# Rotary embedding on a full DMA queue: groups of four batches, half-row tiles, and one PSUM tile for two rows

## The chip, the cores and the metric

The kernel runs on one core of a Trainium2 chip. The metric is the device time of one execution in microseconds; the kernel before takes 162.35 us in the median of 10 runs (162.23 to 162.76).

## The reference

The input x has 16 batches of 512 positions of 1024 numbers in float32. The 1024 numbers are 16 heads of 64, and a head is two halves of 32. Each position has 32 cosines and 32 sines, which all batches and heads share.

```python
x = x.reshape(batch, seq, num_heads, head_dim)
x1, x2 = (x[..., :half_dim].copy(), x[..., half_dim:].copy())
cos = cos[None, :, None, :].copy()
sin = sin[None, :, None, :].copy()
rotated = np.concatenate([x1 * cos - x2 * sin, x1 * sin + x2 * cos], axis=-1)
```

So every output element is its own input times a cosine plus the element of the other half times a sine with a sign: two products and a sum for each of 8.4 million elements, 33.5 MB in and 33.5 MB out.

## The kernel before

**Tiles.** A tile is two batches (`NB = 2`): partition p holds 8 consecutive positions ("rows" of 1024 numbers) of one batch, 32 KB in one piece in memory and on the chip. There are 8 tiles of 4 MB. Five of them have a place on the chip at once, in buffers for 1, 2 and 2 tiles (`HOMES`); results overwrite the input in place. Tiles 5, 6 and 7 reuse the places of 0, 1 and 2.

**Transfers.** All but one are issued by SP, in program order, on one queue; sin is issued by ACT. First come three rows of tile 0, cos, the other five rows (`FIRST`), tile 1, tile 2, and tiles 3 and 4 in one. After that `stores(t)` at the end of each tile issues what is due: store t, except that tiles 3 and 4 go out together after tile 4; after tile 2 also the load of tile 5 and a load of 6 and 7 together. A DMA that must wait for an engine or for an earlier DMA holds up all that is behind it on SP.

**Tables.** cos and sin come in on 64 partitions and are spread to both batches by a matmul with a 0/1 matrix (`spread`, L121 and L122). `sns` holds each sine with both signs in on-chip memory (L124, L125); the cosines stay in PSUM (`tab`). `own_t` is a copy of row 0's signed sines in PSUM.

**The work on a tile** is written out by hand in order (`manual_schedule`), and each engine executes its instructions in that order. The eight rows go three ways:
- Rows 1-2, 4-5 and 6-7 are the pairs. DVE multiplies a pair with the cosines into the PSUM tile `pd` (L149, `pair_product`), POOL multiplies the swapped halves with the sines into a buffer b (L173, `sin_rows`), and DVE adds the two into x (L197, `pair_sum`). There is one `pd`, of four banks, and so a pair's sum must be done before the next pair's product.
- Row 0: DVE writes the cosine product into the PSUM tile `own_ps` (one tile ahead), multiplies the row by the sines in place (L158, `own_product`); TensorE adds the swapped row to `own_ps` by matmuls with the identity (L184, `pe_add`); ACT copies `own_ps` to x (L217).
- Row 3 (`ROW_PE`) goes in two halves through a PSUM tile of its own, `pe_ps`: DVE's product of 512 (L149), TensorE's addition of POOL's product b3 (L184), ACT's copy (L189), all in `pe_half`.

On DVE a tile is this sequence: product of pair 1, own product, sum of pair 1, first half of row 3, product of pair 2, sum of pair 2, second half of row 3, product of pair 3, row 0's product of the next tile, sum of pair 3. Buffers b come from one pool of three, which also held the tables at the start.

[...]

Of the kernel before, what the change touches and what calls it, by code (L numbers as in the profile page):

```python
# [12 lines left out]
NB = 2  # L13

HOMES = (1, 2, 2)
BANK = 512
# [6 lines left out]
FIRST = (3, 8)  # L23
# [3 lines left out]
def kernel(  # L27
# [12 lines left out]

    nc = tc.nc
# [6 lines left out]
    KK = seq // PB  # L48
    NT = batch // NB
    F = KK * dim  # L50

    x_v = x.rearrange("(t b) (p k) d -> t (b p) (k d)", b=NB, k=KK)
    out_v = out.rearrange("(t b) (p k) h d -> t (b p) (k h d)", b=NB, k=KK)
    cos_v = cos.rearrange("(p k) j -> p (k j)", k=KK)
    sin_v = sin.rearrange("(p k) j -> p (k j)", k=KK)
# [3 lines left out]
    bp = ctx.enter_context(tc.tile_pool(name="bp", bufs=3))  # L59
    pfix = ctx.enter_context(tc.tile_pool(name="pfix", bufs=1, space=bass.MemoryType.PSUM))  # L60
# [4 lines left out]

    homes = [xp.tile([P, n, F], FP32, name=f"x{n}{i}") for i, n in enumerate(HOMES)]
    places = [home[:, i] for home, n in zip(homes, HOMES) for i in range(n)]
    tiles = [places[t % len(places)] for t in range(NT)]
    first_of = [sum(HOMES[:i]) for i in range(len(HOMES))]

    def both(t):

        return homes[first_of.index(t % len(places))]

    def load(t, lo=0, hi=KK):
        s = slice(lo * dim, hi * dim)
        nc.sync.dma_start(out=tiles[t][:, s], in_=x_v[t][:, s])

    def load_two(t):
        nc.sync.dma_start(out=both(t), in_=x_v[t : t + 2].rearrange("t p f -> p t f"))  # L80

    def store(t):
        nc.sync.dma_start(out=out_v[t], in_=tiles[t])  # L83

    def store_two(t):
        nc.sync.dma_start(out=out_v[t : t + 2].rearrange("t p f -> p t f"), in_=both(t))

    tabs = bp.tile([P, 2 * dim], FP32, name="b")
    sin_sb = tabs[:PB, : KK * half]
    cos_sb = tabs[:PB, dim : dim + KK * half]  # L90
    nc.scalar.dma_start(out=sin_sb, in_=sin_v)
    load(0, 0, FIRST[0])
    nc.sync.dma_start(out=cos_sb, in_=cos_v)
    for lo, hi in zip(FIRST, FIRST[1:]):
        load(0, lo, hi)
    load(1)
    load(2)
    load_two(3)
# [3 lines left out]
    for _ in range(2):  # L102
        nc.gpsimd.nop(hint="pause")
# [3 lines left out]
    pe_ps = pe.tile([P, BANK], FP32)  # L107
    for ps in (own_ps[:, :BANK], own_ps[:, BANK:], pe_ps):
        nc.tensor.matmul(out=ps, lhsT=zero[:, :P], rhs=zero, start=True, stop=True)  # L109

    sns = fixed.tile([P, KK, 2, half], FP32)
    tab = pfix.tile([P, BANK], FP32)
    cos_t = tab[:, : KK * half]
    sin_t = pd.tile([P, 2 * dim], FP32, name="pd")[:, : KK * half]
# [8 lines left out]
    sin_k = sin_t.rearrange("p (k j) -> p k j", k=KK)  # L123
    nc.vector.tensor_scalar_mul(out=sns[:, :, 0, :], in0=sin_k, scalar1=-1.0)  # L124
    nc.vector.tensor_copy(out=sns[:, :, 1, :], in_=sin_k)  # L125
    own_t = tab[:, KK * half : KK * half + hd]
    nc.vector.tensor_copy(out=own_t, in_=sns[:, ROW_OWN])
# [8 lines left out]
    def rows(t, k, n=1):  # L136
        return tiles[t][:, k * dim : (k + n) * dim]

    def cos_product(out, r, k, n=1):

        c = cos_t[:, k * half : (k + n) * half]
        m = r.shape[1] // (n * half)
        if n == 1:
            cb = bass.AP(tensor=c.tensor, offset=c.offset, ap=[c.ap[0], [0, m], [1, half]])
            o, i = (z.rearrange("p (a j) -> p a j", j=half) for z in (out, r))
        else:
            cb = bass.AP(tensor=c.tensor, offset=c.offset, ap=[c.ap[0], [half, n], [0, m], [1, half]])
            o, i = (z.rearrange("p (k a j) -> p k a j", k=n, j=half) for z in (out, r))
        nc.vector.tensor_tensor(out=o, in0=i, in1=cb, op=ALU.mult)  # L149

    def own_product(r):

        s = bass.AP(
            tensor=own_t.tensor,
            offset=own_t.offset + half,
            ap=[own_t.ap[0], [0, nh], [-half, 2], [1, half]],
        )
        nc.vector.tensor_tensor(out=heads(r), in0=heads(r), in1=s, op=ALU.mult)  # L158

    def sin_product(out, r, k, n):  # L160
# [14 lines left out]
    def sin_rows(t, k, n):  # L175
        b = bp.tile([P, 2 * dim], FP32, name="b")[:, : n * dim]
        sin_product(b, rows(t, k, n), k, n)
        return b
# [7 lines left out]
    def pe_half(k, r, b):  # L186
        cos_product(pe_ps, r, k)
        pe_add(pe_ps, b)
        nc.scalar.copy(out=r, in_=pe_ps)  # L189

    def pair_product(t, k):
        ps = pd.tile([P, 2 * dim], FP32, name="pd")
        cos_product(ps, rows(t, k, 2), k, 2)
# [5 lines left out]
    def stores(t):  # L199
        if t == 4:  # L200
            store_two(3)
        elif t != 3:
            store(t)
        if t == 2:
            load(5)
            load_two(6)

    cos_product(own_ps, rows(0, ROW_OWN), ROW_OWN)
    for t in range(NT):
        first, second, third = PAIRS  # L210
        b1 = sin_rows(t, first[0], 2)
        p1 = pair_product(t, first[0])
        r0 = rows(t, ROW_OWN)
        own_product(r0)
# [6 lines left out]
        h0, h1 = zip(parts(rows(t, ROW_PE)), parts(b3))  # L221
        pe_half(ROW_PE, *h0)
        p2 = pair_product(t, second[0])
        b1 = sin_rows(t, third[0], 2)
        pair_sum(*p2, b2)
        pe_half(ROW_PE, *h1)
        p1 = pair_product(t, third[0])
        if t + 1 < NT:
            cos_product(own_ps, rows(t + 1, ROW_OWN), ROW_OWN)
# [37 lines left out]
```

## Time and profile before

| | |
|---|---|
| median of 10 runs | 162.35 us |
| the profiled execution's own time | 162.4 us |
| its span, first to last instruction | 160.6 us |
| DVE busy | 136.4 us (85%) |
| POOL busy | 127.0 us (79%) |
| PE busy / ACT busy | 60.9 us / 18.8 us |
| moved by DMA | 67.25 MB, 419 GB/s over the span |
| DVE pair products, L149, 24 of 128x2048 | 2291 ns each |
| DVE pair sums, L197, 24 of 128x2048 | 2287 ns each |
| POOL products, L173, 24 of 128x2048 and 8 of 128x1024 | 4524 and 2354 ns each |
| DVE products into own_ps and own products, 8 of each | 1224 and 1214 ns each |
| DVE half products of row 3, 16 | 686 ns each |
| ACT copies of row 0 and of half of row 3 | 1012 and 586 ns each |

A line of a group or of the timeline names the line of the kernel, the engine, the operation, the tile written and the tiles read, and the shapes. In a timeline the first number is the start and the second the duration in us; "x3" says that several instructions are merged in a line, and brackets hold the idle time of the engine before it and what ended it. "SPq" is SP's queue of instructions that issue DMAs. In the view of 40 slices each digit is the busy share of a fortieth of the span in tenths. Instructions of one engine overlap by up to 0.1 us at their ends, so the distance from start to start is what counts on a busy engine: 2.20 us for a pair's product or sum, 1.13 for a full row, 0.60 for a half row.

### The profile page before, as it was taken

Reading aid. Unit: us, or ns where it says so; the run is one execution under the profiler, and the core shown is the slowest. Engines: PE = TensorE matmul, PEld = TensorE weight load, DVE = VectorE, ACT = ScalarE, POOL = GpSimd, SP = SyncE. Lnnn points to the kernel's source line nnn. Section 1 sums busy time; section 2 is a strip of 40 time slices with the busy share of each in tenths; the row PEclk is TensorE's granted clock in tenths of the full one; section 3 lists DMA queues with packets and bytes.
Section 4 is the critical chain, followed back from the end, with each engine's and each line's share of the span. In section 5 each row is a group of like instructions: output and inputs, shape, how many; then the busy total and the mean of one; then the engine's idle time right before and its main releaser. Section 6 shows DMA issues by size and latency. Waiting matters only on the chain.

```text
span 160.6 us, 431 instructions
## 1 busy us (share of the span) xinstructions
PE 60.9 (38%) x71; PEld 19.2 (12%) x71; DVE 136.4 (85%) x85; ACT 18.8 (12%) x25; POOL 127.0 (79%) x38
## 2 busy tenths in 40 slices
PE   3043904074505740393119330844057502922000
PEld 0112200030102110220013000300021101210000
DVE  1079879999999999999999999998999999998000
ACT  0003211003100300021101210031003010211000
POOL 1059999999999999988998699982999999960000
PEclk9999995558655675558555955586556755585555
DMA  5999999999999999999999999999999999999993
GB/s 178 410 418 463 400 490 416 392 457 457 392 424 473 408 400 498 408 392 484 424 400 457 449 400 424 482 392 416 482 408 408 482 416 408 473 424 400 441 457 147
DMA packets 2561, 67.25 MB, mean 419 GB/s; under 512 B 256, under 2 KB 384, under 8 KB 384
## 3 DMA queue, kind: packets, MB, share of 16 engines
q1 hardware_dynamic: 2480, 67.18, 97.9%
q10 hardware_dynamic: 80, 0.07, 0.1%
q14 instruction: 1, 0.01, 0.0%
HBM read 33.69 MB, written 33.55 MB: 419 GB/s over the span
## 4 chain that ended last, share of the span: by engine, by line
DVE 43%; DMA 34%; issue 7%; POOL 7%; PE 1%; DVEq 0%; SPq 0%
DVE x L197 21%; DVE pd L149 18%; DMA x<-in_x_dram 18%; DMA out_dram<-x 12%; POOL b L173 7%; DMA b<-in_sin_dram 4%; DVE pe_ps L149 2%; PE pd L121 1%; DVE sns L124 0%; DVE sns L125 0%; DVE own_ps L149 0%; DVE x L158 0%; DVEq L197 0%; SPq L80 0%; SPq L83 0%
## 5 line engine op out<-in xcount | busy, mean ns | idle before, releaser
L173 POOL TENSOR_TENSOR b<-x,sns 128x2048 f32<-128x2048 f32 (+1 forms) x32 | 126.3, 3982 | 15.4 <-DVE sns L125 8.4
L197 DVE TENSOR_TENSOR x<-pd,b 128x2048 f32<-128x2048 f32 x24 | 54.9, 2287 | 2.3 <-POOL b L173 1.5
L149 DVE TENSOR_TENSOR pd<-x,tab 128x2048 f32<-128x2048 f32 x24 | 55.0, 2291 | 0.2
L184 PE MATMUL own_ps<-x,ident 128*128 128x512 f32 x32 | 30.2, 1100 | 54.7 <-DVE x L158 49.7
L184 PE MATMUL pe_ps<-b,ident 128*128 128x512 f32 x32 | 28.9, 1005 | 23.7 <-DVE pe_ps L149 23.7
L184 PEld LDWEIGHTS own_ps<-x,ident 128*128 128x128 f32 x32 | 9.4, 324 | 74.4 <-DVE x L158 60.5
L217 ACT COPY x<-own_ps 128x1024 f32<-128x1024 f32 x8 | 8.1, 1012 | 74.7 <-PE own_ps L184 74.7
L189 ACT COPY x<-pe_ps 128x512 f32<-128x512 f32 x16 | 9.4, 586 | 38.0 <-PE pe_ps L184 38.0
L184 PEld LDWEIGHTS pe_ps<-b,ident 128*128 128x128 f32 x32 | 8.4, 287 | 42.7 <-DVE pe_ps L149 34.1
L149 DVE TENSOR_TENSOR pe_ps<-x,tab 128x512 f32<-128x512 f32 x16 | 11.0, 686 | 0.0
L149 DVE TENSOR_TENSOR own_ps<-x,tab 128x1024 f32<-128x1024 f32 x8 | 9.8, 1224 | 0.5 <-DMA x<-in_x_dram 0.4
L158 DVE TENSOR_TENSOR x<-x,tab 128x1024 f32<-128x1024 f32 x8 | 9.7, 1214 | 0.0
L124 DVE TENSOR_SCALAR sns<-pd 128x256 f32<-128x256 f32 x1 | 0.4, 425 | 7.3 <-PE pd L121 7.3
L121 PE MATMUL pd<-b,spread 64*128 64x256 f32 x2 | 1.2, 696 | 5.0 <-DMA b<-in_sin_dram 5.0
L217 ACT ACT_TABLE_LOAD x1 | 1.3, 1283 | 14.6 <-DVE x L158 14.6
L109 PE MATMUL own_ps<-zero 128*128 128x512 bf16 x2 | 1.0, 620 | 1.2 <-DVE zero L105 1.2
L121 PEld LDWEIGHTS pd<-b,spread 64*128 64x128 f32 x2 | 0.5, 306 | 5.9 <-issue 5.9
L122 PE MATMUL tab<-b,spread 64*128 64x256 f32 x2 | 1.1, 631 | 0.0
L105 DVE MEMSET zero<- 128x256 uint32 x1 | 0.3, 272 | 0.9 <-PEq L248 0.9
L122 PEld LDWEIGHTS tab<-b,spread 64*128 64x128 f32 x2 | 0.7, 333 | 0.2
L109 PE MATMUL pe_ps<-zero 128*128 128x512 bf16 x1 | 0.6, 634 | 0.0
L109 PEld LDWEIGHTS <-zero 128*128 128x128 bf16 x3 | 0.3, 122 | 1.5 <-DVE zero L105 1.2
(9 smaller groups left out, 1.8 us busy)
## 6 DMA issues: line engine op xcount, KB each, us to landing
out_dram<-x SPq DMA_DIRECT2D x6, 4096.0 KB, 22.1
x<-in_x_dram SPq DMA_DIRECT2D x2, 8192.0 KB, 39.1
x<-in_x_dram SPq DMA_DIRECT2D x3, 4096.0 KB, 27.9
out_dram<-x SPq DMA_DIRECT2D x1, 8192.0 KB, 33.3
x<-in_x_dram SPq DMA_DIRECT2D x1, 2560.0 KB, 12.0
x<-in_x_dram SPq DMA_DIRECT2D x1, 1536.0 KB, 6.5
b<-in_sin_dram ACTq DMA_DIRECT2D x1, 64.0 KB, 6.8
b<-in_cos_dram SPq DMA_DIRECT2D x1, 64.0 KB, 6.6
```

What stands on the lines that cost most here:

```text
L105: nc.vector.memset(zero, 0.0)
L109: nc.tensor.matmul(out=ps, lhsT=zero[:, :P], rhs=zero, start=True, stop=True)
L121: nc.tensor.matmul(out=sin_t, lhsT=spread, rhs=sin_sb, start=True, stop=True)
L122: nc.tensor.matmul(out=cos_t, lhsT=spread, rhs=cos_sb, start=True, stop=True)
L124: nc.vector.tensor_scalar_mul(out=sns[:, :, 0, :], in0=sin_k, scalar1=-1.0)
L149: nc.vector.tensor_tensor(out=o, in0=i, in1=cb, op=ALU.mult)
L158: nc.vector.tensor_tensor(out=heads(r), in0=heads(r), in1=s, op=ALU.mult)
L173: nc.gpsimd.tensor_tensor(out=o, in0=i, in1=sb, op=ALU.mult)
L184: nc.tensor.matmul(out=ps, lhsT=ident, rhs=other, start=False, stop=True, skip_group_check=True)
L189: nc.scalar.copy(out=r, in_=pe_ps)
L197: nc.vector.tensor_tensor(out=r, in0=ps, in1=b, op=ALU.add)
L217: nc.scalar.copy(out=r0, in_=own_ps)
```

## The change

A group is now four batches (`NB = 4`), so that a partition has 16 consecutive rows (64 KB in one piece in memory), and a tile is one half of them: tile t is half t % 2 of group t // 2. There are again 8 tiles of 8 rows per partition, 4 MB each. The places are five slots in one buffer `xt`, so that the two tiles of a group lie side by side.

- Transfers: all on SP. Three rows of tile 0, sin, cos, five rows of tile 0, tile 1, tiles 2 and 3 in one, tile 4. Stores: tiles 0 and 1 in one after tile 1, then 2, 3, 4, 5 and 6 alone, and the last in two pieces of four rows (`LAST_OUT`). After tile 2 the load of tile 5 and of 6 and 7 in one, as before.
- Tables: sin and cos have buffers of their own, on 32 partitions, and 512 columns; the spreading matmuls are 512 wide. The second half of `sns` is written by ACT, not by DVE. The cosines fill a bank; `own_t`, for both halves of a group, is in a bank of its own and is written inside tile 0 after the first pair product.
- `pe_ps` and `pe_half` are gone. Row 3 goes whole through `own_ps`, after row 0 of the same tile and before row 0 of the next: one product of 1024, four matmul passes, one copy. On DVE it comes after the product of pair 2.
- The buffers b are two pools: three for pairs, two for row 3.
- The two pauses on POOL at the start and one of three zeroing matmuls are gone.

```diff
-NB = 2
-
-HOMES = (1, 2, 2)
+NB = 4
+SLOTS = 5
...
-FIRST = (3, 8)
+FIRST = 3
+LAST_OUT = 4
...
-    KK = seq // PB
-    NT = batch // NB
+    KK = seq // PB // 2
+    NT = 2 * batch // NB
...
-    x_v = x.rearrange("(t b) (p k) d -> t (b p) (k d)", b=NB, k=KK)
+    x_v = x.rearrange("(g b) (p k) d -> g (b p) (k d)", b=NB, k=2 * KK)
...
+    b1p = ctx.enter_context(tc.tile_pool(name="b1p", bufs=2))
...
+    xt = xp.tile([P, SLOTS * F], FP32)
+
+    def run(t, lo=0, hi=KK):
+
+        a, b = (t % SLOTS) * F, (t % 2) * F
+        return xt[:, a + lo * dim : a + hi * dim], (t // 2, slice(None), slice(b + lo * dim, b + hi * dim))
...
-    tabs = bp.tile([P, 2 * dim], FP32, name="b")
-    sin_sb = tabs[:PB, : KK * half]
-    cos_sb = tabs[:PB, dim : dim + KK * half]
-    nc.scalar.dma_start(out=sin_sb, in_=sin_v)
-    load(0, 0, FIRST[0])
+    load(0, 0, FIRST)
+    sin_sb = fixed.tile([PB, BANK], FP32)
+    cos_sb = fixed.tile([PB, BANK], FP32)
+    nc.sync.dma_start(out=sin_sb, in_=sin_v)
     nc.sync.dma_start(out=cos_sb, in_=cos_v)
-    for lo, hi in zip(FIRST, FIRST[1:]):
-        load(0, lo, hi)
+    load(0, FIRST, KK)
     load(1)
-    load(2)
-    load_two(3)
+    load(2, 0, 2 * KK)
+    load(4)
...
-    for _ in range(2):
-        nc.gpsimd.nop(hint="pause")
...
-    pe_ps = pe.tile([P, BANK], FP32)
-    for ps in (own_ps[:, :BANK], own_ps[:, BANK:], pe_ps):
+    for ps in (own_ps[:, :BANK], own_ps[:, BANK:]):
...
-    sns = fixed.tile([P, KK, 2, half], FP32)
-    tab = pfix.tile([P, BANK], FP32)
-    cos_t = tab[:, : KK * half]
-    sin_t = pd.tile([P, 2 * dim], FP32, name="pd")[:, : KK * half]
+    sns = fixed.tile([P, 2 * KK, 2, half], FP32)
+    cos_t = pfix.tile([P, BANK], FP32)
+    own_t = pfix.tile([P, 2, hd], FP32)
+    sin_t = pd.tile([P, 2 * dim], FP32, name="pd")[:, :BANK]
...
-    nc.vector.tensor_copy(out=sns[:, :, 1, :], in_=sin_k)
-    own_t = tab[:, KK * half : KK * half + hd]
-    nc.vector.tensor_copy(out=own_t, in_=sns[:, ROW_OWN])
+    nc.scalar.copy(out=sns[:, :, 1, :], in_=sin_k)
...
-        b = bp.tile([P, 2 * dim], FP32, name="b")[:, : n * dim]
-        sin_product(b, rows(t, k, n), k, n)
+        b = (bp if n == 2 else b1p).tile([P, n * dim], FP32, name=f"b{n}")
+        sin_product(b, t, k, n)
...
-    def pe_half(k, r, b):
-        cos_product(pe_ps, r, k)
-        pe_add(pe_ps, b)
-        nc.scalar.copy(out=r, in_=pe_ps)
...
     def stores(t):
-        if t == 4:
-            store_two(3)
-        elif t != 3:
+        if t == 1:
+            store(0, 0, 2 * KK)
+        elif t == NT - 1:
+            store(t, 0, LAST_OUT)
+            store(t, LAST_OUT, KK)
+        elif t > 1:
             store(t)
         if t == 2:
             load(5)
-            load_two(6)
+            load(6, 0, 2 * KK)
...
         p1 = pair_product(t, first[0])
+        if t == 0:
+            nc.vector.tensor_copy(out=own_t, in_=sns[:, ROW_OWN::KK].rearrange("p k a j -> p k (a j)"))
         r0 = rows(t, ROW_OWN)
-        own_product(r0)
+        own_product(t, r0)
...
         pair_sum(*p1, b1)
-        h0, h1 = zip(parts(rows(t, ROW_PE)), parts(b3))
-        pe_half(ROW_PE, *h0)
         p2 = pair_product(t, second[0])
+        cos_product(own_ps, t, ROW_PE)
+        for ps, b in zip(parts(own_ps), parts(b3)):
+            pe_add(ps, b)
+        nc.scalar.copy(out=rows(t, ROW_PE), in_=own_ps)
         b1 = sin_rows(t, third[0], 2)
         pair_sum(*p2, b2)
-        pe_half(ROW_PE, *h1)
         p1 = pair_product(t, third[0])
         if t + 1 < NT:
-            cos_product(own_ps, rows(t + 1, ROW_OWN), ROW_OWN)
+            cos_product(own_ps, t + 1, ROW_OWN)
```

## The prediction

> **What bounds the kernel now.** I read the page's 40 slices first, then the DMA queues, then what the SP queue waited for, and last the timeline of one tile and of the start. The DMA row of the slices is full between the first and the last:
>
> ```profile
> DMA  5999999999999999999999999999999999999993
> ...
> q1 hardware_dynamic: 2480, 67.18, 97.9%
> ```
>
> One queue carries 67.18 MB and its packets fill 97.9% of the span on all 16 engines. The packet records of the trace give 1.213 us for a 32 KB packet. The last stores landed at 140.40, 150.07 and 159.75 us: 9.68 us for each 4 MB tile, end to end. So 16 tile transfers fill some 155 us of 160.6; what is left is the start (first packet at 1.73), its ramp, and the 0.83 us after the last landing. The compute engines do not set the end, but they are close behind:
>
> ```profile
> 114.95 33.36 SPq L83 DMA_DIRECT2D out_dram<-x  x3
> ...
> 145.61 2.29 DVE L197 TENSOR_TENSOR x<-pd,b 128x2048 f32<-128x2048 f32 x1
> ```
>
> The last pair sum ends at 147.90 and store 7 is issued then; store 6 lands at 150.07. The DMA never runs dry, by only two microseconds. So what decides is how long DVE takes over a tile. In steady state (tile 2 starts at 46.47, the other tiles look the same) it reads:
>
> ```profile
> 46.47 2.29 DVE L149 TENSOR_TENSOR pd<-x,tab 128x2048 f32<-128x2048 f32 x1
> ...
> 48.67 1.21 DVE L158 TENSOR_TENSOR x<-x,tab 128x1024 f32<-128x1024 f32 x1
> 49.80 2.28 DVE L197 TENSOR_TENSOR x<-pd,b 128x2048 f32<-128x2048 f32 x1
> ...
> 49.94 3.78 PE L184 MATMUL own_ps<-x,ident 128*128 128x512 f32 x4 [6.90 <-DVE x L158]
> ...
> 52.00 0.69 DVE L149 TENSOR_TENSOR pe_ps<-x,tab 128x512 f32<-128x512 f32 x1
> 52.60 2.29 DVE L149 TENSOR_TENSOR pd<-x,tab 128x2048 f32<-128x2048 f32 x1
> ...
> 53.76 1.01 ACT L217 COPY x<-own_ps 128x1024 f32<-128x1024 f32 x1 [10.10 <-PE own_ps L184]
> 54.99 2.29 DVE L197 TENSOR_TENSOR x<-pd,b 128x2048 f32<-128x2048 f32 x1
> ```
>
> DVE has no gap: it goes round in 16.97 us (46.47 to 63.44). POOL needs 3 x 4.52 + 2.35 = 15.9 us. Row 0's path through PE and ACT ends at 54.77, 8.30 after the tile's start, and nobody on DVE waits for it: the next write to `own_ps` comes at 59.99, and row 3 has a bank of its own, `pe_ps`.
>
> **What the Trainium skill says.** "PSUM — Partial Sum Buffer", section "PSUM: the matmul accumulator": 8 banks of 2 KiB per partition. Before: `tab` 1, `own_ps` 2, `pe_ps` 1, `pd` 4, all 8. After: `cos_t` 1, `own_t` 1, `own_ps` 2, `pd` 4, again all 8; the wider table took the bank of `pe_ps`. "DMA: Bandwidth & Descriptors", "Issuing engines are not separate DMA queues": transfers share the 16 engines whoever issues them. The trace agrees: sin, issued on ACT at 0.73, lands at 7.50 among the others. The same page, "Latency and other measured facts", has copies at 207 GB/s for rows 512 KiB apart against 214 for a padded pitch; here rows go from 32 to 64 KiB apart. No row of this trace shows such a pitch.
>
> **The change part by part.**
> *Bytes and packets.* x and out move the same bytes. Three double transfers may become 64 KB packets; comparing 12 KB (0.460), 20 KB (0.762) and 32 KB packets gives 7 ns of fixed cost each, so 384 packets fewer over 16 engines save 0.17 us at most; if the packets stay at 32 KB, nothing. I take nothing.
>
> *The shared `own_ps`.* Row 3's two half products (0.69 each, 0.60 from start to start) become one of 1.22 (1.13 from start to start), saving 0.07. But the product now writes `own_ps`, so it waits until ACT has copied row 0 out; and the next tile's row 0 product waits until ACT has copied row 3 out. From the start of the own product: 1.21 + 0.05 to PE + 3.78 of matmuls + 0.03 + copy 1.01 + about 0.05 to DVE = 6.13. The 0.05 is an estimate, from DVE to PE here. Counted from the same start, DVE begins the pair sum at 1.13, the second pair product 2.32 later, and is free for row 3 another 2.20 later: 5.65. Wait: 0.48. (2.32 and not 2.20, because pair sum and next product now follow each other on the same `pd`, as the third sum and next product did: 44.15 to 46.47.) The second round is alike: 1.22 + 0.05 + 3.78 (four cold matmuls, as row 0 has; before, two took 2.00) + 0.03 + 1.01 + 0.05 = 6.14, against 1.13 + 2.32 + 2.20 = 5.65. Wait: 0.49. Queued behind each wait on DVE are the pair sum and everything after, so the loss is not hidden. The tile is now 2.21 + 6.13 + 6.14 + 1.13 + 2.32 = 17.93 us, 0.96 more than 16.97: without the waits it would be level, since the two added gaps of 0.12 cancel the 0.07 saved and the 0.20 for which the second sum no longer waits on its own product.
>
> *The start.* sin moves from ACT's queue onto SP behind the first load, in one order with cos. It should land like cos now does, 7.72 instead of 7.50. A partition's table now holds 16 rows of 32 frequencies, so each table matmul is 512 wide and not 256. The timeline of the start of before:
>
> ```profile
> 7.64 1.19 PE L121 MATMUL pd<-b,spread 64*128 64x256 f32 x2 [5.00 <-DMA b<-in_sin_dram]
> ...
> 8.62 1.06 PE L122 MATMUL tab<-b,spread 64*128 64x256 f32 x2
> ...
> 9.99 1.23 DVE L149 TENSOR_TENSOR own_ps<-x,tab 128x1024 f32<-128x1024 f32 x1
> ```
>
> A 512-wide pass goes by every 0.853 us in the row 0 group, twice the 0.427 here. Four passes: 7.85 + 3 x 0.853 + 1.06 = 11.5 for cos, so the first product starts at 11.5 and not 9.99 (+1.5). sin is complete at 9.8; scaling it takes about 0.69 (a 512-wide product) beside ACT's copy, 0.59. POOL starts at 10.5 (+0.8) and has its first three results at 15.0, 17.3 and 21.8, ahead of DVE's need (16.3, 21.3, 22.4). The ACT copy's table load, 1.28 us, I cost at nothing: it needs no data and ACT is idle until 9.8. With that cover gone, see the rival below. The removed nops and the smaller zeroing (0.63 of PE at 2.0) lie before sin lands: nothing. The new buffers for b let POOL run further ahead; it waited 2.0 us for DVE in all, so nothing. Copying `own_t` inside tile 0 adds 0.25.
>
> *Compute's end.* Tile 0 starts at 12.63, its own product at 15.09, row 3 at 21.22, next row 0 at 27.36, tile 1 at 30.81 (29.49 before). Tile 7 starts at 30.81 + 6 x 17.93 = 138.39. Its row 3 is out of ACT at 138.39 + 8.34 + 6.09 = 152.82, and store 7a (rows 0 to 3) is issued at 152.9. The last tile has no next row 0, so the last sum ends at 146.73 + 3.45 + 2.40 + 2.28 = 154.86; 7b goes out at 154.9, against 148.0.
>
> *Transfers in between.* Loads of tiles 0 to 4 fill the queue to 52.5. The double store goes out after tile 1, at about 48.8, in time. Store 2 goes at 66.7, the double runs to 71.9. Load 5 waits for the double to land, 71.9, while store 2 transfers; the double load waits for store 2, 82, while load 5 transfers. SP has stores 3 to 7 queued behind these waits, each ready later (84.7, 102.6, 120.5, 138.4). Tiles 2 and 3 land together at 42.9, needed at 45.2; tile 4 at 52.5, needed far later; tiles 6 and 7 at 111.4, needed at 116.8. So nothing starves before store 6, issued at 138.4, done by about 149.8. There is the new hole: 149.8 until 7a's packets.
>
> *Tail.* 152.9 + 1.0 from issue to first packet (0.73 to 1.73 at the start) + ramp 0.55 + 9.68 for both halves + 0.35 to land + 0.83 = 165.3. The ramp is not shown for a store; the first load took 1.1 more than its bytes, so it is 0 to 1.1, and I take the middle. 7b is queued in time. 165.3 against 160.6 is +4.7; on the profiled execution's own 162.4, 167.1. The median is 162.35, so I forecast 167.1.
>
> **The rivals.**
> *The DMA stays the bound.* Then the saturated queue ends as before, at most 0.2 us earlier: 162.2. It decides if DVE's two waits in a tile sum to 0.40 us or less instead of 0.97: the hole of 4.1 us shrinks by 7 us per us of wait per tile. For it speaks the full DMA row and that 2 us of slack plus the split store hide much; against, that the four matmuls and the copy have constant lengths in every tile. 10%, and this is the case that ends not slower.
> *The table load comes late.* If ACT's copy of sin carries a second wait, the load follows it, as now at 14.61 behind a DVE wait. Then POOL starts at about 12.3 (the copy behind DVE's scaling, 10.5 + 1.28 + 0.59), its third result comes at 23.7 and the second sum slips 1.3: 168.4. Against it: both writers of `sns` touch different elements and today run without a wait between them. 12%.
> *The 64 KiB pitch slows the DMA.* A 10% loss costs 15.5 us on 155: about 178. The skill's 207 against 214 speaks against it; a 3.3% loss there gives 5 us, 167.5, no later than my compute chain. 4%.
>
> **How the numbers follow.** Forecast 71%: 165.5 to 168.6 by itself, from the unknown waits (0.10 us for the two in a tile makes 0.7), the ramp (0.55 either way) and the start (0.3). Waits between break-even and my estimate, 163 to 165.5: 3%. The range reaches from 164.8 to 169.2, with the table case in it, and leaves out no change, the pitch and part of the partial case. What a measurement of this kernel can tell from no change is 0.2%, 0.3 us. Faster 3%, from the packet saving in the DMA-bound case; same 7%; slower 90%.
>
> **What would show it.** Right: DVE idle before the `own_ps` products, released by ACT, 15 or 16 times at 0.4 to 0.5 us, some 7 us in all; a tile's period of about 17.9; last sum near 155; a hole in the DMA row near 150 to 154; store 7a queued before 7b with both waiting for compute. Wrong: a period under 17.3; POOL as the releaser of DVE in steady state; a DMA row without the hole; packets longer than 1.22 us per 32 KB; a table load after 9 us.

## The result, and the profile after

The changed kernel takes 164.81 us (median of 9 runs, 164.13 to 165.28) against 162.42 for the kernel before in the same comparison (32 runs, 162.21 to 163.10). The ratio is 1.0141, with a 95% interval of 1.0128 to 1.0153: slower by 2.4 us, where 4.7 were forecast. The profiled execution took 164.38 us, with a span of 162.6; before it was 162.4 and 160.6. So the span grew by 2.0 us.

The page of the kernel after, 40 slices and DMA queue, with the chain that ended last (shares of the span by engine):

```profile
PEclk9999995558585769555855555558555955585555
DMA  5999999699699899889999989979999999995796
...
q1 hardware_dynamic: 2256, 67.24, 96.9%
...
DMA 31%; PE 18%; issue 18%; DVE 15%; ACT 6%; POOL 6%; SPq 0%; ACTq 0%; POOLq 0%; DVEq 0%
```

The chain of the kernel before, in the same order:

```profile
DVE 43%; DMA 34%; issue 7%; POOL 7%; PE 1%; DVEq 0%; SPq 0%
```

The DMA row now has a dent in the two slices before the last two. The queue moves 67.24 MB, sin's now among them, in 2256 packets instead of 2480, and its share of the span fell from 97.9% to 96.9%. In the chain of work that ended last, PE and ACT had 1% and nothing before; they now have 18% and 6%. The row-wise path through TensorE and ACT, which nobody waited for, has moved onto the path that sets the end.

The end of the timeline of the kernel after (start, duration, engine, line, operation), and three windows around it (window, its length, busy us of PE, PEld, DVE, ACT and POOL with counts, granted clock, DMA share, GB/s), with the first of the three in the kernel before below them:

```profile
150.55 2.88 SPq L82 DMA_DIRECT2D out_dram<-xt  x2
150.78 2.29 DVE L182 TENSOR_TENSOR xt<-pd,b 128x2048 f32<-128x2048 f32 x1
```

```profile
148.00:150.00 2.00, 1.43 (x2) 0.00 (x0) 1.97 (x2) 0.49 (x1) 0.00 (x0) 0.50 0.31 131
150.00:152.00 2.00, 0.00 (x0) 0.00 (x0) 1.90 (x2) 0.52 (x1) 0.00 (x0) 0.50 0.33 139
152.00:154.00 2.00, 0.00 (x0) 0.00 (x0) 1.07 (x1) 0.00 (x0) 0.00 (x0) 0.50 1.21 508
```

```profile
148.00:150.00 2.00, 0.00 (x0) 0.00 (x0) 0.00 (x0) 0.00 (x0) 0.00 (x0) 0.50 0.69 295
```

The last sum ends at 153.07, not at 147.90 as before. Most of the 16 DMA engines have moved their part of store 6 by about 149.3 (the slowest one's part lands at 150.83), store 7a is issued at 150.55, and its first packet moves at 151.38. In between most of the DMA is dry for about 2.1 us, about as much as the span grew. Before, the window 148 to 150 still had a DMA share of 0.69 and the next one 1.19.

One tile of the kernel after (tile 4) in the timeline; the bracket at the end of a line holds the idle time before it and what ended it:

```profile
83.55 2.29 DVE L140 TENSOR_TENSOR pd<-xt,cos_t 128x2048 f32<-128x2048 f32 x1
...
87.07 3.75 PE L174 MATMUL own_ps<-xt,ident 128*128 128x512 f32 x4 [8.10 <-issue]
...
90.86 1.01 ACT L207 COPY xt<-own_ps 128x1024 f32<-128x1024 f32 x1 [10.80 <-PE own_ps L174]
91.90 1.23 DVE L140 TENSOR_TENSOR own_ps<-xt,cos_t 128x1024 f32<-128x1024 f32 x1 [0.41 <-ACT xt L207]
...
93.28 3.75 PE L174 MATMUL own_ps<-b,ident 128*128 128x512 f32 x4 [2.46 <-DVE own_ps L140]
...
98.16 1.23 DVE L140 TENSOR_TENSOR own_ps<-xt,cos_t 128x1024 f32<-128x1024 f32 x1 [0.50 <-ACT xt L215]
...
101.61 2.30 DVE L140 TENSOR_TENSOR pd<-xt,cos_t 128x2048 f32<-128x2048 f32 x1
```

This tile went as forecast: two rounds of matmuls, copy and product in series, DVE waiting for ACT by 0.41 and 0.50 us, and a period of 101.61 - 83.55 = 18.06 us where 17.93 were forecast. In the next tile row 3 did not:

```profile
111.39 2.36 PE L174 MATMUL own_ps<-b,ident 128*128 128x512 f32 x4 [2.50 <-DVE own_ps L140]
...
113.83 1.01 ACT L215 COPY xt<-own_ps 128x1024 f32<-128x1024 f32 x1 [3.85 <-PE own_ps L174]
...
115.67 1.22 DVE L140 TENSOR_TENSOR own_ps<-xt,cos_t 128x1024 f32<-128x1024 f32 x1
```

Here the same four matmuls took 2.36 us instead of 3.75. The copy was done at 114.84, DVE came at 115.67, and there was no wait. Two windows with the columns as above show what differs between the two groups:

```profile
93.00:97.00 4.00, 3.72 (x4) 1.17 (x4) 3.97 (x3) 0.00 (x0) 4.00 (x1) 0.50 1.21 524
111.00:114.00 3.00, 2.36 (x4) 0.68 (x4) 2.97 (x3) 0.17 (x1) 1.78 (x1) 0.80 1.01 437
```

The granted TensorE clock is 0.50 of full under the first group and a mean of 0.80 under the second: it was full from 109.38 to 112.80. So DVE waits less for ACT than was forecast (us in total, times, longest; only idle times over 0.15 us are listed):

```profile
DVE own_ps L140 <- ACT xt L207: 2.5, 6, 0.4
...
DVE own_ps L140 <- ACT xt L215: 0.8, 2, 0.5
```

Eight waits, not 15 or 16. Six follow row 0, whose group took 3.6 us or more in six of eight tiles. Two follow row 3, in the only tiles where its group took over 3.5 us. The list understates the loss: it leaves out short waits, and an instruction that waits also loses its overlap of about 0.1 us with the one before. Counted from start to start against the 2.20 us of an undisturbed pair product, the 15 products into `own_ps` that follow one start 4.7 us late in all; the forecast's 0.48 and 0.49 make 7.3.

### The profile page after: what moved, and what is told of

It reads as the page before. It is cut to its first block, busy times and chain, and to the rows that moved or that the text cites. A ratio compares the mean times of both kernels' runs of the same rounds, so it can differ in the third digit from the quotient of the medians.

```text
span 162.6 us, 421 instructions
## 1 busy us (share of the span) xinstructions
PE 59.1 (36%) x70; PEld 18.0 (11%) x70; DVE 137.7 (85%) x76; ACT 18.1 (11%) x18; POOL 126.8 (78%) x38
## 3 DMA queue, kind: packets, MB, share of 16 engines
q1 hardware_dynamic: 2256, 67.24, 96.9%
## 4 chain that ended last, share of the span: by engine, by line
DMA 31%; PE 18%; issue 18%; DVE 15%; ACT 6%; POOL 6%; SPq 0%; ACTq 0%; POOLq 0%; DVEq 0%
PE own_ps L174 17%; DMA out_dram<-xt 15%; DMA xt<-in_x_dram 12%; DVE xt L182 7%; POOL b L163 6%; DMA sin_sb<-in_sin_dram 4%; DVE pd L140 4%; ACT xt L207 3%; ACT xt L215 3%; DVE own_ps L140 2%; PE pd L112 1%; DVE xt L146 1%; DVE sns L115 0%; ACT sns L116 0%; SPq L78 0%
## 5 line engine op out<-in xcount | busy, mean ns | idle before, releaser
L163 POOL TENSOR_TENSOR b<-xt,sns 128x2048 f32<-128x2048 f32 (+1 forms) x32 | 126.1, 3982 | 16.3 <-ACT sns L116 10.5
L140 DVE TENSOR_TENSOR pd<-xt,cos_t 128x2048 f32<-128x2048 f32 x24 | 55.1, 2295 | 0.8
L182 DVE TENSOR_TENSOR xt<-pd,b 128x2048 f32<-128x2048 f32 x24 | 54.8, 2285 | 0.1
L174 PE MATMUL own_ps<-xt,ident 128*128 128x512 f32 x32 | 29.2, 1069 | 63.2 <-issue 33.5
L174 PE MATMUL own_ps<-b,ident 128*128 128x512 f32 x32 | 25.1, 929 | 19.8 <-DVE own_ps L140 19.8
L140 DVE TENSOR_TENSOR own_ps<-xt,cos_t 128x1024 f32<-128x1024 f32 x16 | 19.6, 1228 | 4.6 <-ACT xt L207 2.5
L174 PEld LDWEIGHTS own_ps<-xt,ident 128*128 128x128 f32 x32 | 9.4, 324 | 83.4 <-issue 76.8
L207 ACT COPY xt<-own_ps 128x1024 f32<-128x1024 f32 x8 | 8.1, 1012 | 85.6 <-PE own_ps L174 85.6
L215 ACT COPY xt<-own_ps 128x1024 f32<-128x1024 f32 x8 | 8.1, 1012 | 37.0 <-PE own_ps L174 31.8
L174 PEld LDWEIGHTS own_ps<-b,ident 128*128 128x128 f32 x32 | 7.4, 252 | 37.3 <-issue 25.2
L146 DVE TENSOR_TENSOR xt<-xt,own_t 128x1024 f32<-128x1024 f32 x8 | 9.7, 1215 | 0.0
```

The lines of the kernel that those rows point to most:

```text
L163: nc.gpsimd.tensor_tensor(out=o, in0=i, in1=sb, op=ALU.mult)
L174: nc.tensor.matmul(out=ps, lhsT=ident, rhs=other, start=False, stop=True, skip_group_check=True)
L182: nc.vector.tensor_tensor(out=r, in0=ps, in1=b, op=ALU.add)
L207: nc.scalar.copy(out=r0, in_=own_ps)
L215: nc.scalar.copy(out=rows(t, ROW_PE), in_=own_ps)
```

## The experiments

"After" is the changed kernel and "before" the one it was made from. Times are medians; a ratio is always to the kernel before on the same chip.

**Copying row 0 and row 3 in halves.**

```diff
-nc.scalar.copy(out=r0, in_=own_ps)
+for ps, r in zip(parts(own_ps), parts(r0)):
+    nc.scalar.copy(out=r, in_=ps)
```

and the same for row 3, on top of after.

> Theory (the two rows that share one PSUM tile make DVE wait for ACT, and the lost time opens a hole in the DMA before the last store): ACT's copy of each row in two halves, the first beside TensorE's second half, ends 0.43 us earlier (0.59 after the last matmul instead of 1.01). A wait of 0.45 falls to about 0.05, the tile period to about 17.05 us, row 3 of the last tile is out at about 147, before the DMA queue is empty at 149.3, and the hole is gone: span 160.4, time 162.2 to 162.5. Rival (the new layout, 64 KB apart in memory, or the order of the transfers makes the DMA itself slower): the time stays at 164.4 to 164.8.

Measured: 165.79 us (165.30 to 166.40), ratio 1.0218 (1.0188 to 1.0248), so 1.0 us slower than after. From its timeline:

```profile
17.09 3.75 PE L174 MATMUL own_ps<-xt,ident 128*128 128x512 f32 x4 [5.02 <-POOL b L163]
...
20.88 1.07 ACT L208 COPY xt<-own_ps 128x512 f32<-128x512 f32 x2 [9.17 <-PE own_ps L174]
```

The first half copy did not start behind the second matmul but behind the fourth, at 20.88. Nothing overlapped, and two copies take 1.07 where one took 1.01. The idea missed, but the chain became 0.06 longer, DVE waited 4.7 us for ACT instead of 3.3, and the time went the same way.

**The last store in one piece.**

```diff
-store(t, 0, LAST_OUT)
-store(t, LAST_OUT, KK)
+store(t)
```

> Theory: the last tile goes out in one transfer, so it waits for the last pair sum (153.07 in the changed kernel) and not for row 3 (150.5). The hole of 2.1 us grows by 2.5: 167.0 to 167.4. Rival (the DMA queue is the bound and never empties): no change, 164.4 to 164.8.

Measured: 166.96 us (166.82 to 167.53), ratio 1.0295 (1.0275 to 1.0315). The DMA share in the windows 148 to 150, 150 to 152 and 152 to 154 is 0.23, 0.00 and 0.00: the hole now lasts until the last sum is done. In the changed kernel the two pieces are worth 2.15 us, since half of the last tile leaves while DVE still works on the other half.

**The tables loaded ahead of the first piece of x.**

```diff
-load(0, 0, FIRST)
 nc.sync.dma_start(out=sin_sb, in_=sin_v)
 nc.sync.dma_start(out=cos_sb, in_=cos_v)
+load(0, 0, FIRST)
```

> Theory: sin and cos are issued ahead of the first load and land at about 3 us, so that the tables are ready when the first rows land, at about 8. DVE's first product starts at about 8.5 instead of 12.1, all tiles are 3.5 us earlier, row 3 of the last tile is out at about 147 and the hole closes: 162.3 to 162.8. Rival (a later start is made up for on the way, the tile period alone counts): 164.4 to 164.8.

Measured: 164.02 us (163.40 to 164.72), ratio 1.0108 (1.0076 to 1.0141). The first product starts at 8.08 instead of 12.09. Of these 4 us, 2.0 reach tile 1, which starts at 29.08. The timeline of this run shows where the rest went:

```profile
21.10 2.29 DVE L182 TENSOR_TENSOR xt<-pd,b 128x2048 f32<-128x2048 f32 x1 [2.32 <-POOL b L163]
```

POOL is behind in tile 0, since its input, row 3 of x, landed later. Store 7a went out at 148.03 and the hole was gone. The time still stayed 1.7 us above before: the DMA share in the windows 0 to 2 and 2 to 4 us is 0.11 and 0.74, where after has 0.40 and 0.76, which makes 0.6 us of lost DMA time, and the last engine landed store 6 at 151.02. An earlier start of compute helps only until the DMA is the bound again, and here it was bought with DMA time.

**Row 3 in a bank of its own, in the changed kernel.** A bank for `pe_ps` was to be had only by giving up `own_t`: the sines of row 0 come from SBUF again.

```diff
-o = own_t[:, t % 2]
+o = sns[:, ROW_OWN + t % 2 * KK].rearrange("p a j -> p (a j)")
...
-cos_product(own_ps, t, ROW_PE)
+pe_half(t, 0, h0)
...
+pe_half(t, 1, h1)
```

> Row 3 goes again in two halves through a PSUM tile of its own; the bank for it is freed by reading row 0's sines from on-chip memory instead of from PSUM. Theory: no wait of DVE for ACT, tile period 16.97, last sum at about 148.5, no hole, 162.2 to 162.5. Rival one (DMA slower by the layout): 164.4 to 164.8. Rival two (DVE's own product with both operands outside PSUM gets in the way of POOL): POOL's products longer than 4.52 us or own products longer than 1.21 us, and the period above 17.2.

Measured: 180.36 us (179.54 to 180.47), ratio 1.1101. One row of its costliest groups (count, busy us, mean ns):

```profile
L146 DVE TENSOR_TENSOR xt<-xt,sns 128x1024 f32<-128x1024 f32 x8 | 28.1, 3517 | 0.0
```

With its table in PSUM the same product takes 1215 ns. The Trainium skill, "SBUF — State Buffer", section "SBUF: two separate sides", says that DVE and GpSimd share a port pair as an exclusive lock, and that a DVE operation with two SBUF inputs and a GpSimd operation that reads SBUF block each other fully. This run agrees: 3.52 us against 1.21 in the mean, and in all eight tiles DVE's product ends 1.08 us after the end of the POOL product that was running when it began (in tile 4 at 98.04, after 96.96). The cost of this side effect buries the question, so the run decides nothing on sharing `own_ps`. Sharing had to be tried on the kernel before.

**Each half copy directly behind its half's matmuls, `own_ps` still one tile of two banks.**

```diff
 for ps, r in zip(parts(own_ps), parts(r0)):
     pe_add(ps, swapped(r))
-nc.scalar.copy(out=r0, in_=own_ps)
+    nc.scalar.copy(out=r, in_=ps)
```

and the same for row 3, on top of after.

> The changed kernel with each half copy of rows 0 and 3 written directly behind the matmuls of its half, so that ACT's first copy needs only those. In the run with the half copies behind the whole group both copies began after the fourth matmul (20.88 after 20.84) and the pair took 1.07 instead of 1.01. Theory (DVE's wait for ACT): the first copy now runs beside the second half's matmuls, a row leaves its PSUM tile 0.4 us earlier, the waits of 0.45 nearly vanish, the period falls to 17.0 to 17.2, and the hole before the last store closes: span 160.6 to 161.6, time 162.4 to 163.2. Rival (the tile's copies cannot be parted, or DVE waits for something else): 164.4 to 166.

Measured: 178.20 us (178.09 to 178.28), ratio 1.0979 (1.0963 to 1.0996). From the timeline of the run:

```profile
62.40 2.05 PE L174 MATMUL own_ps<-b,ident 128*128 128x512 f32 x2 [2.03 <-DVE own_ps L140]
...
64.49 0.58 ACT L215 COPY xt<-own_ps 128x512 f32<-128x512 f32 x1 [3.49 <-PE own_ps L174]
...
65.12 2.07 PE L174 MATMUL own_ps<-b,ident 128*128 128x512 f32 x2 [0.67 <-ACT xt L215]
...
67.85 1.23 DVE L140 TENSOR_TENSOR own_ps<-xt,cos_t 128x1024 f32<-128x1024 f32 x1 [1.07 <-ACT xt L215]
```

The second pair of matmuls writes the other bank, and yet it waits until ACT has read the first: the program orders accesses by the whole two-bank tile. TensorE loses 0.67 us there, and from one product into `own_ps` to the next it now takes 6.82 us (61.03 to 67.85), where tile 4 of after takes 6.26 (91.90 to 98.16). DVE waited 1.0 to 1.1 us 15 times, and the period grew to 19.25. A part of the 13 us over after has another reason: in this run every pair of matmuls took 2.04 to 2.08 us, so that none was at full clock. As an attempt to shorten the chain it failed. As a test it says that 0.6 us more in the chain costs as much on DVE each time: 19.25 is twice 0.6 above the 18.06 of tile 4, whose groups were all at half clock too.

**One part alone: row 3 through `own_ps`, everything else as before.**

```diff
-h0, h1 = zip(parts(rows(t, ROW_PE)), parts(b3))
-pe_half(ROW_PE, *h0)
+cos_product(own_ps, rows(t, ROW_PE), ROW_PE)
+for ps, b in zip(parts(own_ps), parts(b3)):
+    pe_add(ps, b)
+nc.scalar.copy(out=rows(t, ROW_PE), in_=own_ps)
...
-pe_half(ROW_PE, *h1)
```

> The kernel before with one part of the change: row 3 goes whole through own_ps; layout, transfers and tables stay. Theory: waits of 0.3 to 0.5 us of DVE for ACT, tile period 17.3 to 17.9, last tile starts at 133 to 137 instead of 131.9, store 7 (one piece) goes out 1.5 to 5 us later than 148.0 and the DMA has a hole before it: 163.3 to 166.5. Rival (the late start alone makes the loss): 162.2 to 162.6, no hole.

Measured: 165.08 us (164.97 to 165.30), ratio 1.0173 (1.0158 to 1.0188). This one edit costs 2.7 us, a little more than the whole change (2.4), in which the last store goes out in two pieces. DVE waits for ACT by 2.5 us in six and 0.8 in two waits, the same as in after. The last sum ends at 150.85 instead of 147.90, and the window 148 to 150 of this run shows the hole (DMA share next to last):

```profile
148.00:150.00 2.00, 0.00 (x0) 0.00 (x0) 1.90 (x2) 0.35 (x1) 0.00 (x0) 0.50 0.08 33
```

**The same, with TensorE kept busy.** If short groups are short because of the clock, then a TensorE that always works should make all of them short. 6 and 30 matmuls of zeros into the now unused `pe_ps` follow the two rows' copies in program order:

```diff
+def keep_busy(n):
+    for _ in range(n):
+        nc.tensor.matmul(out=pe_ps, lhsT=zero[:, :P], rhs=zero, start=True, stop=True)
...
+keep_busy(6)
...
+keep_busy(30)
```

> As the kernel before with the shared own_ps, and TensorE is kept busy between its groups: 6 zero matmuls of 512 bf16 columns after row 0's group and 30 after row 3's, into the PSUM tile that is free. Theory (the length of the four matmuls follows the granted clock: 3.75 us at half, 2.36 at full, and it was the clock that made the waits shorter than forecast): clock near 1.0, groups of 2.4 to 2.6 us, no wait of DVE for ACT, period 17.0, no hole: 162.2 to 162.6. Rival (the clock does not matter to fp32 groups, as the prediction took it): groups stay at 3.75 and the time is that of the run before it or more, 163.3 or above.

Measured: 164.37 us (164.10 to 164.48), ratio 1.0125 (1.0110 to 1.0140), mean clock 0.914 instead of 0.651. From the timeline:

```profile
84.70 1.95 PE L184 MATMUL own_ps<-x,ident 128*128 128x512 f32 x4 [1.68 <-DVE x L158]
...
88.99 1.22 DVE L149 TENSOR_TENSOR own_ps<-x,tab 128x1024 f32<-128x1024 f32 x1
```

At full clock the four matmuls take 1.95 us and DVE does not wait. (The 2.36 us that was expected came from a group at a mean clock of 0.80.) Six of the 16 groups still took 3.06 to 3.75 us: one before the first clock record, five where the clock had fallen back. DVE's listed waits for ACT shrink from 3.3 to 1.2 us, but it now waits 1.1 us for the load of tiles 6 and 7, which lands at 112.75 instead of 111.54. The last sum ends at 149.26, 1.6 us earlier than in the run before this. Only 0.7 us of that reach the time, so the time expected was missed: the hole shrinks to about 1.0 us, but the last DMA engine lands store 6 at 151.47, 2.6 us after the first; in the kernel before, 1.1 us lay between them.

This program has 1000 instructions instead of 431, and its trace has three packets of 16 KB of the kind "instruction", about 1 us each, at 44.4, 94.2 and 146.5 us; the run before this has none of that size. The distance from the first engine's landing to the last one's goes from 0.5 to 2.3 us between the landings at 33 and at 54 us, so around the first of them, and hardly changes around the other two. That the fetching of instructions disturbs the DMA is argued and not shown. That the clock sets the length of the group, and the group the wait, is shown.

**A late start alone: both table matmuls done twice.**

```diff
-nc.tensor.matmul(out=sin_t, lhsT=spread, rhs=sin_sb, start=True, stop=True)
+for _ in range(2):
+    nc.tensor.matmul(out=sin_t, lhsT=spread, rhs=sin_sb, start=True, stop=True)
```

and the same for cos, on top of before.

> The kernel before with its table matmuls done twice (the same result), as long as 512-wide ones: cos is ready about 1.7 us later and sin 0.85, DVE's first product starts at about 11.7 instead of 10.0, and tile 1 at 30.3 to 31.2 instead of 29.5. Theory: only some 1.3 us of that fits into the slack before the last store, so 162.3 to 163.2. Rival (the start is worth its full 1.5 us): 163.6 to 164.

Measured: 162.29 us, ratio 0.9994 (0.9982 to 1.0006): nothing. The first product starts at 11.71 instead of 9.99. The row 0 product of tile 6 shows where the delay ends, in the timeline of before and of this run:

```profile
111.46 1.23 DVE L149 TENSOR_TENSOR own_ps<-x,tab 128x1024 f32<-128x1024 f32 x1 [0.45 <-DMA x<-in_x_dram]
```

```profile
111.78 1.22 DVE L151 TENSOR_TENSOR own_ps<-x,tab 128x1024 f32<-128x1024 f32 x1
```

DVE used to wait 0.45 us there for a load. Half of the delay is gone before: the second sum of tile 0 used to wait 1.50 us for POOL and now waits 0.65, so that tile 1 starts 0.87 late. These two waits leave 0.32, and the slack before the last store takes that; the last sum ends at 148.22 against 147.90.

**The late start together with the shared `own_ps`** (the two edits above, on top of before).

> The kernel before with two parts together: row 3 through own_ps, and the table matmuls done twice (the start 1.7 us later). Alone the first took 165.08 and the second 162.29, no more than before. Theory (the late start is hidden alone, since the DMA's slack and the wait for tile 6 take it up, and counts in full once the waits have used the slack): 166.4 to 167.0. Rival (the late start is hidden by something that the waits don't touch): 165.0 to 165.4.

Measured: 167.50 us (166.46 to 167.66), ratio 1.0302. The late start that cost nothing alone costs 2.4 us here: the waits have used up the slack, and most of the DMA is dry from about 149 to beyond 154. The two costs do not add up from single runs; they share one slack. It came out somewhat above what was expected: tile 1 starts 1.9 us later than with sharing alone (30.84 against 28.95), and another 0.8 us comes from later tiles, since in this run the first window at full clock comes only at 55.9 us and the groups up to there take 3.70 to 3.75 us. So a part of the 2.4 is the clock's and not the start's. With it the whole change adds up roughly: 162.4, +2.7 for sharing, +2.4 for the late start on top, -2.15 for the two pieces of the last store, makes 165.3 against 164.8 measured.

**The two pieces alone, on the kernel before.**

```diff
-store(t)
+store(t, 0, 4)
+store(t, 4, KK)
```

for the last tile.

> The kernel before with its last store in two pieces of four rows. Theory (the DMA is the bound there and both pieces are queued before store 6 is done): no difference that can be measured, 162.2 to 162.5. Rival (16 KB packets or the additional transfer cost something at the end): up to 163.

Measured: 162.47 us, ratio 1.0006 (0.9997 to 1.0016): nothing. Where the queue never runs dry, an earlier store only waits longer in it.

**`own_ps` as two tiles of one bank**, so that products, matmuls and copies go bank by bank, on top of after. This is the chain of the forecast cut in half.

```diff
-own_ps = pe.tile([P, dim], FP32)
+own_ps = [pe.tile([P, BANK], FP32, name=f"own{i}") for i in range(2)]
...
-nc.scalar.copy(out=r0, in_=own_ps)
+for ps, r in zip(own_ps, parts(r0)):
+    pe_add(ps, swapped(r))
+    nc.scalar.copy(out=r, in_=ps)
```

> The changed kernel with the two banks of own_ps as two tiles of their own: DVE's row product in two halves of 512 (0.60 from start to start, 0.07 more than one of 1024, twice per tile), TensorE's matmuls and ACT's copy bank by bank. In the run before, with one tile and the copies in between, TensorE's second half waited for ACT's first copy (2.05 + 0.6 + 2.07 a row); two tiles take that wait away. Theory: at half clock a row's second bank is free 0.05 + 3.78 + 0.03 + 0.59 + 0.05 = 4.5 us after its product, DVE wants it after some 5: no wait for ACT, period 17.1, last tile at about 134, its row 3 out at 147 to 148, no hole. What is left over the kernel before is only the later landing of the slowest DMA engine: span 160.6 to 161.5, time 162.4 to 163.3. Rival (something beside the waits makes the tile longer): period 17.3 or more, 164 or more.

Measured: 163.09 us (162.60 to 163.53), ratio 1.0042 (1.0027 to 1.0057), 1.7 us faster than after. From its timeline, the starts of three tiles and, in the second of them, how row 0 ends and row 3 begins:

```profile
31.11 2.30 DVE L140 TENSOR_TENSOR pd<-xt,cos_t 128x2048 f32<-128x2048 f32 x1
...
48.20 2.30 DVE L140 TENSOR_TENSOR pd<-xt,cos_t 128x2048 f32<-128x2048 f32 x1
...
53.80 0.59 ACT L215 COPY xt<-own 128x512 f32<-128x512 f32 x1 [9.63 <-PE own L182]
...
56.06 1.29 DVE L148 TENSOR_TENSOR own<-xt,cos_t 128x512 f32<-128x512 f32 x2
...
56.89 3.75 PE L182 MATMUL own<-b,ident 128*128 128x512 f32 x4 [1.42 <-DVE own L148]
...
65.29 2.29 DVE L140 TENSOR_TENSOR pd<-xt,cos_t 128x2048 f32<-128x2048 f32 x1
```

The first bank is copied while TensorE fills the second. From tile 1 on every group takes 3.75 us, at half clock, and still DVE never waits for ACT: the period is 17.09 or 17.10 in each tile, against up to 18.06 in after. So the waits were a matter of the chain through one tile, and not of TensorE's rate alone. The last sum ends at 149.73. What keeps it 0.7 us above before is the DMA, which never runs dry: its slowest engine lands the first load at 7.69, store 6 at 150.67 and the last store at 160.38, where before has 7.28, 150.07 and 159.75. Why it lags is open.

**The two tiles, and sin and cos issued on ACT's queue.**

```diff
-nc.sync.dma_start(out=sin_sb, in_=sin_v)
+nc.scalar.dma_start(out=sin_sb, in_=sin_v)
```

and the same for cos.

> The kernel with two tiles for own_ps (163.09, 0.7 over the kernel before, with no wait of DVE left and its last sum at 149.7) with sin and cos issued on ACT's queue. What is open is that 0.7: its slowest DMA engine lands the first load at 7.7 instead of 7.3 and carries the delay to the last store. If it comes from the small table packets that stand in SP's queue between the two first loads, the slowest engine is back at 7.3 to 7.5 and the time at 162.3 to 162.7. If it comes from the layout (rows 64 KB apart, 32 partitions of tables) or from elsewhere, the time stays at 162.9 to 163.3.

Measured: 162.66 us (162.44 to 163.07) against 162.21 for before, ratio 1.0030 (1.0017 to 1.0042). That is 0.45 us above before, where the two tiles alone were 0.71 above it; the two intervals overlap, so the gain is not clear of the noise. The time lies in the first of the two ranges, but the reason given for it is not what the trace shows: the slowest engine lands the first load at 8.00, later than 7.69. What shrank is the distance from the first engine to the last, from 1.26 to 0.64 us in the first load and from 1.70 to 1.03 in store 6. Nor does the edit change the queue alone: sin now lands at 4.82, and the first product starts at 9.97 instead of 12.04. The remaining 0.3% are left open. No version here beats the kernel before.

## Why the prediction was right in direction and wrong in size

**What held.** Sharing `own_ps` puts TensorE and ACT on DVE's path: shown by the waits of after, and by the one edit that costs 2.7 us alone. The hole before store 7a opened where it was forecast, with 7a and 7b both issued late. The late start costs something once the slack is gone (2.4 us) and nothing before (0.9994). The double transfers move 64 KB packets, 384 of them, at a median of 2.42 us where two 32 KB packets take 2 x 1.213: no gain and no loss, as taken.

**The step that failed** is "3.78 of matmuls" in the sum of each round, held for "constant lengths in every tile". Its wait of 0.97 us per tile and the period of 17.93 follow from it. The group of row 3 took 2.97, 3.21, 3.30, 3.58, 3.75, 2.36, 2.80 and 3.13 us in tiles 0 to 7; that of row 0 took 3.73, 3.49, 3.39, 3.75 four times, and 3.60. With these in the forecast's own formula (a round is the larger of 5.65 and the group plus 2.35 or 2.36), tiles 1 to 6 take 17.15, 17.06, 17.70, 17.87, 17.41 and 17.41 us. The trace has 17.26, 17.26, 17.94, 18.06, 17.51 and 17.51. The pattern over the tiles is there, and 0.1 to 0.24 us in each is left, in hand-overs between engines: from DVE to TensorE 0.05 was set, and it takes 0.10 to 0.15.

So six periods took 105.54 us instead of 107.58: -2.98 by the matmuls' lengths, +0.94 by the hand-overs. The second error hid a third of the first.

The trace of before had the clue, and I read past it. Row 0's groups there do take 3.75 to 3.78 us in all eight tiles, but row 3's pairs of matmuls do not agree with each other. From the timeline of before, the second pair in tiles 1, 2 and 5:

```profile
40.96 2.08 PE L184 MATMUL pe_ps<-b,ident 128*128 128x512 f32 x2 [2.89 <-DVE pe_ps L149]
...
57.94 2.00 PE L184 MATMUL pe_ps<-b,ident 128*128 128x512 f32 x2 [2.84 <-DVE pe_ps L149]
...
108.86 1.73 PE L184 MATMUL pe_ps<-b,ident 128*128 128x512 f32 x2 [2.70 <-DVE pe_ps L149]
```

The pair gets shorter by 0.09 us per tile, and the first pairs lie at 1.5 to 1.7 us. The prediction takes "four cold matmuls" for row 3 and gives no reason why they should stay cold when the period changes; it should have asked why these pairs are not at 2.08. The clock row of before could also mislead:

```profile
PEclk9999995558655675558555955586556755585555
```

It shows 9 in the first six slices, and row 0's first group, 3.75 us at 14.64, lies there. But the first clock record of that trace is at 20.50, and the row shows full where there is none; at full clock the group takes 1.95.

The Trainium skill, "TensorE: Matmul & The Clock Gate", section "What's actually happening", has what was missing: the clock is either half or full, set by TensorE's activity in free-running windows of 3413 ns. The trace agrees: full stretches in after are 3.41 us long (109.38 to 112.80), and half stretches are multiples of that. It also fits the constant lengths of before: five windows are 5 x 3.413 = 17.07 us, and a tile took 16.97, so that each tile met the windows in nearly the same phase, 0.1 us earlier in a window from tile to tile, close to the 0.09 by which the pair changes. The clock records of before show it: full windows end at 40.98, 58.05 and 109.25, and the three pairs above start 0.02, 0.11 and 0.39 us before these ends. The version with two tiles has a period of 17.09 and groups of 3.75 in every tile from tile 1 on. After, with periods of 17.26 to 18.06, meets the windows in another phase each time, and some of its groups fall into full ones. No run set the period on purpose, so this reading of the constancy is argued from the numbers and not tested by itself; that the clock makes the difference between 3.75 and 1.95 is shown.

**The rest of the miss, by place.** The span was forecast at 165.3 and measured at 162.6:

| step | forecast | measured | difference |
| --- | --- | --- | --- |
| start of tile 1 | 30.81 | 31.09 | +0.28 |
| six periods | 107.58 | 105.54 | -2.04 |
| start of tile 7 to issue of 7a | 14.51 | 13.92 | -0.59 |
| issue of 7a to the end | 12.4 | 12.05 | -0.35 |

The third row is mainly the same cause: the last group took 3.13 us. The fourth: the first packet came 0.83 us after the issue instead of 1.0, and the ramp, set at 0.55, was about 0.3 (9.98 us from the first packet of 7a to the end of the last of 7b, against 9.68).

**The start** was right by less than it seems. From the timeline of after:

```profile
0.73 1.28 ACT L116 ACT_TABLE_LOAD   x1 [0.73 <-PEq L239]
...
8.30 2.04 PE L112 MATMUL pd<-sin_sb,spread 32*128 32x512 f32 x2 [6.08 <-DMA sin_sb<-in_sin_dram]
...
10.38 0.69 DVE L115 TENSOR_SCALAR sns<-pd 128x512 f32<-128x512 f32 x1 [8.83 <-PE pd L112]
11.11 0.59 ACT L116 COPY sns<-pd 128x512 f32<-128x512 f32 x1 [9.09 <-DVE sns L115]
11.78 4.51 POOL L163 TENSOR_TENSOR b<-xt,sns 128x2048 f32<-128x2048 f32 x1 [10.47 <-ACT sns L116]
12.09 1.23 DVE L140 TENSOR_TENSOR own_ps<-xt,cos_t 128x1024 f32<-128x1024 f32 x1 [1.01 <-PE cos_t L113]
```

The table load sits at 0.73, as taken, and the rival with a late one fell. But ACT's copy did wait for DVE's scaling, which I had put beside it, so POOL starts at 11.78 and not at 10.5. It did not hurt, since POOL's results were still early enough. That both writers of `sns` ran without a wait in the kernel before was no evidence against such a wait: both are on DVE there (L124, L125). sin landed at 8.17 instead of 7.72, which moves the first product to 12.09 instead of 11.5. Half of that came back within tile 0, where row 3's group took 2.97 us and not 3.78.

**The rivals.** "The DMA stays the bound" fell: the hole is there. It put the break-even at 0.40 us of waiting per tile. The waits listed, 3.3 us over eight tiles, come to 0.41, at which the hole should have been almost closed. But the forecast counted from start to start, and so counted the two products of a tile are late by 0.62 us in the mean of tiles 1 to 6, which is all that the period grew by (105.54 / 6 - 16.97). By the forecast's rule, 7 us of hole for 1 us of waiting per tile, that leaves 4.1 - 7 x (0.97 - 0.62) = some 1.6 us of hole; it is 2.1 us wide. The pitch fell, by the packet times above.

## What to carry to other kernels

A wait is worth only what is left of it after the slack, and several edits draw on the same slack: cost them together, not one by one. When an accumulator tile is used for two rows in turn, its round trip (product, matmuls, copy, next product) must fit into the work that DVE has in between; splitting it into tiles of one bank cuts the trip, while splitting the copies within one tile lengthens it. Before a matmul group's duration is put into a sum, compare it over all tiles and against the granted clock in its own window: in a kernel where TensorE works in short bursts, one group can take 1.95 or 3.75 us.

## What the runs showed of the hardware

- Four fp32 matmuls of 512 columns take 1.95 us at full clock and 3.75 at half. In a kernel whose TensorE is busy for a third of the span, both occur, and everything between. With a period of 16.97 or 17.09, near five windows of 3.41 us, the lengths hardly changed from tile to tile; with 17.26 to 18.06 they did. That the period decides which length a group gets is a reading of these numbers; no run set it on purpose.
- The clock row of a page reads full before the first clock record, while the matmuls there run at half speed. The run with the copies in between has no clock record at all: its mean clock reads 1.000, and its pairs of matmuls take 2.04 to 2.08 us.
- A matmul into one bank of a two-bank PSUM tile waited, by the program's own semaphores, until ACT had read the other bank: 0.67 us in each row, in a run of 178.20 us where after has 164.81 (a part of the difference is that run's half clock). With two tiles of one bank no such wait is left (163.09).
- A DVE product of 128x1024 with both inputs in SBUF, begun while a POOL product ran, ended 1.08 us after that product in all eight tiles: 1.66 to 5.43 us, mean 3.52, where it takes 1.21 with one input in PSUM.
- The 16 DMA engines do not end together. Store 6 lands over 1.1 us in the kernel before, 1.8 in after and 2.6 in the run with 1000 instructions. In the version with two tiles the queue never runs dry, and it is the slowest engine that lands the last store 0.63 us later than before (160.38 against 159.75).
